# Stick-breaking attention: TensorE's products in the order of the source, the opening's V transposes between filling products, ScalarE's side steps tied to fixed places

## The chip, the core and the metric

The kernel runs as one program on one core of a Trainium2 chip. The metric is the device time of one execution in microseconds (us), as a median over runs. The core has five engines with a queue each: TensorE (PE; its weight loads stand apart as PEld), VectorE (DVE), ScalarE (ACT), GpSimd (POOL) and SyncE (SP), which issues most of the DMAs. An engine takes the instructions of its queue in the queue's order, and an instruction that waits on a semaphore holds up what stands behind it.

## The reference

One decoder layer over 1024 positions of width 1024, in float32. The input is normalized, scaled and shifted by a conditioning vector (adaLN), and projected once into all that follows. Two attention families run beside each other: native sparse attention (NSA) and stick-breaking attention; both are projected up, mixed by sigmoid gates, projected out and added; then comes an MLP. The change lies in the stick-breaking part:

```python
def stick_breaking_attention(q, k, v):
    ...
    def block(i):
        start = i * SB_QBLOCK
        t = start + jnp.arange(SB_QBLOCK)
        qb = lax.dynamic_slice_in_dim(q, start, SB_QBLOCK, axis=1)
        z = jnp.einsum('bqhd,bshd->bhqs', qb, k).astype(jnp.float32) * scale
        mask = key_pos[None, :] < t[:, None]
        log_keep = jnp.where(mask, jax.nn.log_sigmoid(-z), 0.0)
        suffix = lax.cumsum(log_keep, axis=3, reverse=True) - log_keep
        a = jnp.where(mask, jnp.exp(jax.nn.log_sigmoid(z) + suffix), 0.0)
        return jnp.einsum('bhqs,bshd->bqhd', a.astype(v.dtype), v)
```

So a weight is sigmoid(z) times the product of sigmoid(-z) over all later keys up to the query: a running product along each row of scores, for 8 heads of 64 channels.

## The kernel before, in words

**Stages.** Normalization, projections, NSA, stick-breaking, up-projection and gates, output projection, MLP. TensorE's operands are split into a high and a low part that it multiplies in separate products, so that three products make one of float32 accuracy. The last columns of the big input projection (the gates) aren't needed before the up-projection. They are cut into 28 units of 48 products (`unit_mm`, line 761, tiles `pd`, weights `uwh` and `uwl`), and their products fill TensorE between the dependent products of the two attention stages: the *filling products*, or fills. `drive` runs an attention generator and, after each step, takes as many fills as the step's cost times a ratio asks for; `pump` takes fills for a stretch of time. Line 1051 copies a finished unit out (`zo`), and line 63 and 66 split the next weights.

**Stick-breaking** (`sb_gens`). For each of 8 heads there are three groups of four chunks: the query blocks 3 to 0 with all their keys (512, 384, 256 and 128 columns), the blocks 7 to 4 with the 512 columns up to the diagonal, and the same blocks with the columns before (512, 384, 256 and 128). One step takes one chunk:
- TensorE makes the scores in a PSUM bank `psx`, of which there are three: Q with the high part of K (line 1156), with the low part (1157), and the causal mask as a further product (1159).
- ScalarE takes two sigmoids of the bank: `sig` (1161), and in place of the scores sigmoid(-z) (1162).
- VectorE runs the product along the row as a scan (1171, into `Pt`), one step later. The scan is what frees the `psx` bank. GpSimd multiplies `sig` by it (1173).
- A group later, TensorE transposes the weights (1188, into `pt`, two banks), ScalarE and VectorE split them into `th` (1196) and `tl` (1197), and TensorE multiplies them by V (1208, one bank `po`).
- At the end of a group of outputs, 1212 and 1214 add the two halves of `po`.

**Side work.** ScalarE, GpSimd and SyncE work beside this on 32 pieces of the MLP's adaLN weights (`ada_rest`: a DMA at line 436, a scaling on ScalarE at 456, an addition on GpSimd at 460). For the next head, Q is cast on ScalarE (1108), its lower half is corrected on GpSimd (1113), and K is split on GpSimd (63, 66). For each pair of heads TensorE transposes V (1126), and ScalarE and VectorE split it (1130, 1132).

**What sets the order.** A scheduler puts each engine's instructions in order when the program is built: of those that its model holds ready, it takes the one of highest priority. Edges added by hand that only order (no semaphore) bind it. `track` notes the last product of an attention step, and `behind` ties a fill behind it; before the change, that was done for one fill in six (`m % 6 == 0`). Everything else, the fills in between and ScalarE's side steps included, moved where the scheduler saw room. In the change, line numbers go up by 7 to 18 from line 427 on: the products of line 761 stand at 776, the scores at 1174, 1175 and 1177, the transposes at 1206, the V products at 1226, the Q cast at 1126, the V transposes at 1144, the adaLN scaling at 463.

Of the kernel before, what the change touches and what calls it, by code (L numbers as in the profile page):

```python
# [6 lines left out]
F32 = mybir.dt.float32  # L7
F32R = mybir.dt.float32r
BF16 = mybir.dt.bfloat16
AF = mybir.ActivationFunctionType  # L10
# [9 lines left out]
HD = 64  # L20
# [15 lines left out]
def build(tc, I, out):  # L36
    nc = tc.nc
# [74 lines left out]
    ones = const.tile([128, 128], F32, name="ones")  # L112
# [311 lines left out]
            nc.scalar.copy(csrc[which][:, h * 512:(h + 1) * 512], cb[which][h])  # L424


    def ada_rest(pool_, rows, ahead, engines, W=512):
        groups = [(r, h) for r in rows for h in range(D // W)]
        total = len(groups) * NK
        nxt = []  # L430

        def load(n):
            r, h = groups[n // NK]
            raw = pool_.tile([128, W], F32, name="adraw", bufs=ahead)
            c0 = (2 + r) * D + h * W
            nc.sync.dma_start(raw, ada_k[:, n % NK, c0:c0 + W])
            nxt.append(raw)

        for n in range(min(ahead, total)):
            load(n)  # L440
        yield
        for n in range(total):
            raw = nxt.pop(0)
            k = n % NK
            (r, h), w, e = groups[n // NK], cs[:, k:k + 1], engines[n // NK % len(engines)]
            if k == 0:
                acc = pool_.tile([128, W], F32, name="adacc", bufs=1)
            if e == "v":
                if k == 0:
                    nc.vector.tensor_scalar(acc, raw, w, None, op0=OP.mult)  # L450
                else:
                    nc.vector.scalar_tensor_tensor(acc, raw, w, acc, op0=OP.mult, op1=OP.add)
            else:
                d = acc if k == 0 else raw
                if e == "s":
                    nc.scalar.mul(d, raw, w)
                else:
                    nc.gpsimd.tensor_scalar(d, raw, w, 0.0, op0=OP.mult, op1=OP.add)
                if k:
                    nc.gpsimd.tensor_tensor(acc, acc, raw, op=OP.add)  # L460
            if n + ahead < total:
                load(n + ahead)
            if k == NK - 1:
                nc.sync.dma_start(acc_d[r][:, h * W:(h + 1) * W], acc)
            yield
# [271 lines left out]

    MM = 0.216

    last, free = [], [0]  # L740

    def track(ins):

        last[:] = [ins.ins]

    def behind(ins):

# [4 lines left out]
    def unit_mm(w, sink):  # L752
        wh, wl = w
        pend = None
        for h in range(2):
            sl = slice(h * 512, (h + 1) * 512)
            p = pd()
            m = 0
            for k in range(NK):
                for n, (a, b) in enumerate(((wh[:, k], uH(k, sl)), (wh[:, k], ul[:, k, sl]), (wl[:, k], uH(k, sl)))):  # L760
                    r = nc.tensor.matmul(p, a, b, start=(k == 0 and n == 0), stop=(k == NK - 1 and n == 2))  # L761
                    if m % 6 == 0:
                        behind(r)
                    m += 1
                    if m == 3 and pend:
                        sink(*pend)
                        pend = None
                    yield MM
            pend = (h, p)
        sink(*pend)  # L770
# [307 lines left out]
    def pump(fill, us):  # L1078

        free[0] = 1  # L1080
        while us > 0:
            m = next(fill, None)
            if m is None:
                break
            us -= m
        free[0] = 0


    def sb_gens(sp):
        zero = sp.tile([128, 128], F32, name="zero")[:, 0:1]  # L1090
        nc.vector.memset(zero, 0.0)

        def load(u, h):
# [5 lines left out]
        def load_v(p):  # L1099
            vr = sp.tile([128, S], F32, name="vr", bufs=1)  # L1100
            nc.sync.dma_start(vr, z_d[8 + p])
            return vr

        def prep(h, ld):

            qr, kr = ld
            Q = sp.tile([128, S], F32R, name="Q", bufs=2)
            nc.scalar.copy(Q, qr)
            yield
            Kh = sp.tile([128, S], F32R, name="Kh", bufs=2)  # L1110
            hi(Kh, kr, "g")
            yield
            nc.gpsimd.tensor_tensor(Q[HD:], qr[HD:], f(Q)[HD:], op=OP.subtract)
            yield
            yield
            Kl = sp.tile([128, S], F32R, name="Kl", bufs=2)
            lo(Kl, kr, Kh, "g")
            yield Q, Kh, Kl
# [29 lines left out]
        def sb_a(kind, chunk, ops, A, edges):  # L1148

            i, c0, c1 = chunk  # L1150
            Q, Kh, Kl = ops
            w = c1 - c0
            p = psx()
            qs = Q[:, i * 128:(i + 1) * 128]
            diag = kind != 2
            track(nc.tensor.matmul(p[:, :w], qs, Kh[:, c0:c1], start=True, stop=False))
            track(nc.tensor.matmul(p[:, :w], qs, Kl[:, c0:c1], start=False, stop=not diag))
            if diag:
                track(nc.tensor.matmul(p[:, w - 128:w], identr, diagr, start=False, stop=True))
            sig = sp.tile([128, w], F32, name="sigr" if kind == 1 else "sig%d" % w, bufs=5 if kind == 1 else 2)  # L1160
            nc.scalar.activation(sig, p[:, :w], AF.Sigmoid, scale=HD ** -0.5)
            nc.scalar.activation(p[:, :w], p[:, :w], AF.Sigmoid, scale=-(HD ** -0.5))
            A[i, kind] = (sig, c0)

            def fin():
                Pt = sp.tile([128, 640], F32, name="Pt", bufs=6)
                if diag:
                    nc.vector.memset(Pt[:, w:w + 1], 1.0)
                else:
                    nc.vector.tensor_copy(Pt[:, w:w + 1], edges.pop(i)[:, 0:1])  # L1170
                nc.vector.tensor_tensor_scan(Pt[:, 0:w][:, ::-1], p[:, 0:w][:, ::-1], zero.to_broadcast([128, w]),
                                             1.0 if diag else Pt[:, w:w + 1], op0=OP.mult, op1=OP.add)
                nc.gpsimd.tensor_tensor(sig, sig, Pt[:, 1:w + 1], op=OP.mult)
                if kind == 1:
                    edges[i] = Pt
            return fin, max(w, 256) * 2 / 2400.
# [41 lines left out]
        def sb_all():  # L1218
            lds = {0: (load(0, 0), load(4, 0))}
            vr = load_v(0)  # L1220
            ops = {}
            for r in prep(0, lds[0]):
                ops[0] = r
            V = []
            for c in prep_v(vr, V):
                yield c
            groups = [(h, kind) for h in range(8) for kind in range(3)]
            A, edges, late = {}, {}, []
            extra = []
# [143 lines left out]
    fill = fill_all()  # L1373
    pump(fill, 25.0)
    drive(nsa_all(), fill, 0.4, 0.05)
    pump(fill, 20.0)
    close(wp)
    close(at)
    close(bnp)
    close(kvp)  # L1380
    sp = pool("sb", "right")
    ada_steps = ada_rest(sp, (3,), 2, "s", 256)
    drive(sb_gens(sp), fill, 0.55, 0.08, TAIL)
    for _ in ada_steps:
        pass
    close(sp)
# [407 lines left out]
```

## Time and profile before

| | us |
|---|---|
| median of 3 runs (1702.85 to 1706.73) | 1703.29 |
| the profiled execution | 1704.85 |
| its span, first to last instruction | 1703.1 |
| stick-breaking stage within it, first setup steps to last V product | 612 to 847 |
| TensorE busy in the span | 1636.8 |
| TensorE busy in the 235 us of that stage | 218.29 |

Times in the views are microseconds from the start of the span. A matmul row gives its start, its duration and the operand shapes; durations of successive matmuls overlap, so the pace is read from the distance of their starts. The name in brackets behind a row is the event that ended the idle time just before it. The clock in a windows row is the share of TensorE's full clock that was granted, over that window.

### The profile page before, as it was taken

Reading aid. Unit: us, or ns where it says so; the run is one execution under the profiler, and the core shown is the slowest. Engines: PE = TensorE matmul, PEld = TensorE weight load, DVE = VectorE, ACT = ScalarE, POOL = GpSimd, SP = SyncE. Lnnn points to the kernel's source line nnn. Section 1 sums busy time; section 2 is a strip of 40 time slices with the busy share of each in tenths; the row PEclk is TensorE's granted clock in tenths of the full one; section 3 lists DMA queues with packets and bytes.
Section 4 is the critical chain, followed back from the end, with each engine's and each line's share of the span. In section 5 each row is a group of like instructions: output and inputs, shape, how many; then the busy total and the mean of one; then the engine's idle time right before and its main releaser. Section 6 shows DMA issues by size and latency. Waiting matters only on the chain.

```text
span 1703.1 us, 25878 instructions
## 1 busy us (share of the span) xinstructions
PE 1636.8 (96%) x8484; PEld 1377.4 (81%) x8484; DVE 1273.8 (75%) x2614; ACT 873.9 (51%) x1898; POOL 950.7 (56%) x837
## 2 busy tenths in 40 slices
PE   6999999999999989999999999989999999999998
PEld 5879888888888867878778887768788888888886
DVE  7698478778777557878655557569888888979897
ACT  6433476667666456766554435534444443454442
POOL 0021143434434268775326303399889897989897
PEclk9999999999999999999999999999999999999999
DMA  9465344444543474441187543855363554636232
GB/s 304 109 198 157 110 142 156 128 149 143 166 131 125 130 196 128 115 125 59 36 301 232 165 151 127 292 212 210 134 262 116 231 211 148 251 113 268 98 148 99
DMA packets 195103, 279.87 MB, mean 164 GB/s; under 512 B 19401, under 2 KB 145049, under 8 KB 186009
## 3 DMA queue, kind: packets, MB, share of 16 engines
q1 hardware_dynamic: 190744, 276.13, 48.8%
q10 hardware_dynamic: 4224, 2.10, 0.4%
q8 instruction: 67, 1.10, 0.3%
q14 instruction: 68, 0.55, 0.1%
HBM read 203.71 MB, written 39.86 MB: 143 GB/s over the span
## 4 chain that ended last, share of the span: by engine, by line
PE 73%; POOL 8%; DMA 6%; DVE 6%; issue 3%; ACT 3%; SPq 1%; POOLq 0%; DVEq 0%; ACTq 0%
PE pd L761 15%; PE psx L1734 10%; PE pd L1668 7%; PE pt L1668 5%; PE px L1357 5%; PE po L955 4%; PE px L1470 4%; PE po L1734 3%; POOL raw L1708 3%; PE pt L975 2%; PE psx L844 2%; DMA adraw<-in_ada_w_dram 2%; PE psx L845 2%; POOL wbl L1710 1%; PE psx L603 1%
## 5 line engine op out<-in xcount | busy, mean ns | idle before, releaser
L1737 DVE TENSOR_TENSOR acc<-acc,psx 128x512 f32<-128x512 f32 x288 | 178.7, 675 | 9.8 <-PE psx L1734 9.7
L761 PE MATMUL pd<-uh,uwh 128*128 128x512 f32 x448 | 181.2, 404 | 0.7 <-ACT zo L1051 0.7
L761 PE MATMUL pd<-ul,uwh 128*128 128x512 f32 x448 | 177.4, 396 | 0.0
L761 PE MATMUL pd<-uh,uwl 128*128 128x512 f32 x448 | 177.1, 395 | 0.0
L66 DVE TENSOR_TENSOR wl<-aw,wh 128x1024 fp32r<-128x1024 f32 x49 | 114.6, 2339 | 63.9 <-ACT wh L61 63.9
L1708 POOL TENSOR_TENSOR raw<-r 128x512 f32<-128x512 f32 x80 | 132.5, 1675 | 32.1 <-ACT r L1643 32.0
L1734 PE MATMUL psx<-wbl,rah 128*128 128x512 f32 x336 | 131.3, 391 | 5.9 <-POOL wbl L1710 4.6
L1734 PE MATMUL psx<-wbh,rah 128*128 128x512 f32 x336 | 130.6, 390 | 1.9 <-ACT wbh L1709 1.5
L1734 PE MATMUL psx<-wbh,ral 128*128 128x512 f32 x336 | 130.9, 390 | 0.1
L947 DVE TENSOR_TENSOR tl<-pt,th 128x512 fp32r<-128x512 f32 (+8 forms) x168 | 103.5, 619 | 32.9 <-ACT th L946 31.4
L946 ACT CAST th<-pt 128x512 fp32r<-128x512 f32 (+8 forms) x168 | 88.9, 533 | 68.2 <-PE pt L975 67.0
L1710 POOL TENSOR_TENSOR wbl<-raw,wbh 128x1024 fp32r<-128x1024 f32 x40 | 108.9, 2724 | 19.5 <-ACT wbh L1709 19.5
L63 POOL TENSOR_SCALAR uwh<-uwr 128x512 fp32r<-128x512 f32 x54 | 34.3, 645 | 136.0 <-PE pd L761 115.9
L1696 POOL TENSOR_TENSOR w<-w,grow 128x1024 f32<-128x1024 f32 x32 | 95.0, 2992 | 11.8 <-DVE aw L1624 11.8
L1709 ACT CAST rah<-raw 128x1024 fp32r<-128x1024 f32 x40 | 41.5, 1051 | 113.9 <-PE po L1734 60.7
L761 PEld LDWEIGHTS pd<-uh,uwl 128*128 128x128 f32 x448 | 84.9, 189 | 17.2
L761 PEld LDWEIGHTS pd<-uh,uwh 128*128 128x128 f32 x448 | 85.2, 190 | 14.9 <-ACT zo L1051 1.1
L901 POOL TENSOR_TENSOR pcx<-pcx,tot 128x64 f32<-128x64 f32 (+7 forms) x32 | 11.5, 359 | 153.5 <-ACT Pn L864 40.8
L761 PEld LDWEIGHTS pd<-ul,uwh 128*128 128x128 f32 x448 | 85.1, 190 | 14.0
L1668 PE MATMUL pd<-mth,wh 128*128 128x512 f32 x224 | 87.3, 390 | 0.9 <-ACT wh L61 0.9
L1668 PE MATMUL pd<-mth,wl 128*128 128x512 f32 x224 | 87.1, 389 | 0.9 <-DVE wl L66 0.9
L1668 PE MATMUL pd<-mtl,wh 128*128 128x512 f32 x224 | 87.2, 389 | 0.0
(359 smaller groups left out, 5326.3 us busy)
## 6 DMA issues: line engine op xcount, KB each, us to landing
mtl<-t_d SPq DMA_DIRECT2D x35, 1024.0 KB, 5.7
mth<-t_d SPq DMA_DIRECT2D x35, 1024.0 KB, 8.2
w<-in_mlp_w_dram SPq DMA_DIRECT2D x32, 512.0 KB, 5.5
z_d<-zo SPq DMA_DIRECT2D x56, 256.0 KB, 2.3
Pr<-Pn SPq DMA_DIRECT2D x112, 128.0 KB, 2.0
aw<-in_mlp_w_dram SPq DMA_DIRECT2D x28, 512.0 KB, 4.0
uwr<-in_w_in_dram SPq DMA_DIRECT2D x54, 256.0 KB, 3.2
adraw<-in_ada_w_dram SPq DMA_DIRECT2D x48, 256.0 KB, 3.1
```

The source lines that it names most:

```text
L66: (nc.vector if e == "v" else nc.gpsimd).tensor_tensor(dst, src, f(h), op=OP.subtract)
L761: r = nc.tensor.matmul(p, a, b, start=(k == 0 and n == 0), stop=(k == NK - 1 and n == 2))
L946: nc.scalar.copy(th[:rows, :w], p[:rows, :w])
L947: nc.vector.tensor_tensor(tl[:rows, :w], p[:rows, :w], f(th)[:rows, :w], op=OP.subtract)
L955: track(nc.tensor.matmul(po_[:, :256], w, tt[q][:rows, m * 256:(m + 1) * 256], start=(n == 0 and m == 0 and q == 0), stop=(n == last and m ...
L1357: nc.tensor.matmul(p, a, b, start=(k == 0 and n == 0), stop=(k == 3 and n == 2))
L1668: nc.tensor.matmul(bank[ft], a[:, k, fs], b[k], start=(k == 0 and m == 0 and not on), stop=(k == 3 and m == 2), skip_group_check=on)
L1696: nc.gpsimd.tensor_tensor(W2[c][j], W2[c][j], grow2, op=OP.mult)
L1708: nc.gpsimd.tensor_tensor(d, block(i0, j0, s), block(i1, j1, s), op=OP.add if sg > 0 else OP.subtract)
L1710: (nc.vector if e == "v" else nc.gpsimd).tensor_tensor(l.rearrange("p s n -> p (s n)"), src, f(h).rearrange("p s n -> p (s n)"), op=OP.sub ...
L1734: nc.tensor.matmul(p, a[:, s, qs], b[:, s], start=(s == 0 and n == 0), stop=(s == 1 and n == 2))
L1737: nc.vector.tensor_tensor(acc[:, t, ds_], acc[:, t, ds_], p, op=OP.add if sg > 0 else OP.subtract)
```

## The change

Five things change, all for the stick-breaking stage:
- **A strict order for TensorE.** While `strict` isn't None, each product of the stage, every fill included, is tied by an order-only edge behind the one before it in the source. The scheduler can't move them any more.
- **ScalarE's side steps.** The adaLN scaling and the Q cast are tied behind the last sigmoid that the source has issued (`behind_sig`).
- **The opening.** `pump` before the stage takes 4 us of fills in place of 20. Then the generator runs to its first two stops (after the loads and the preparation of head 0, and after V's transposes), with 8 us of fills behind each.
- **An early sigmoid.** One sigmoid of one column comes ahead of the preparation, so ScalarE's sigmoid table is loaded there.
- **Buffers.** The adaLN pieces get four buffers and are loaded four ahead, in place of two.

```diff
     def ada_rest(pool_, rows, ahead, engines, W=512):
...
                 if e == "s":
-                    nc.scalar.mul(d, raw, w)
+                    behind_sig(nc.scalar.mul(d, raw, w))
...
-    last, free = [], [0]
+    last, free, strict = [], [0], [None]
+
+    def chain(ins):
+
+        if strict[0] is not None:
+            if strict[0]:
+                after(ins, strict[0])
+            strict[0] = ins
 
     def track(ins):
 
         last[:] = [ins.ins]
+        chain(ins)
...
                     r = nc.tensor.matmul(p, a, b, start=(k == 0 and n == 0), stop=(k == NK - 1 and n == 2))
-                    if m % 6 == 0:
+                    if strict[0] is not None:
+                        chain(r)
+                    elif m % 6 == 0:
                         behind(r)
...
             Q = sp.tile([128, S], F32R, name="Q", bufs=2)
-            nc.scalar.copy(Q, qr)
+            behind_sig(nc.scalar.copy(Q, qr))
...
-            nc.scalar.activation(p[:, :w], p[:, :w], AF.Sigmoid, scale=-(HD ** -0.5))
+            sig_last[0] = nc.scalar.activation(p[:, :w], p[:, :w], AF.Sigmoid, scale=-(HD ** -0.5))
...
             vr = load_v(0)
+
+            nc.scalar.activation(warm, ones[:, 0:1], AF.Sigmoid)
             ops = {}
             for r in prep(0, lds[0]):
                 ops[0] = r
+            yield 0.0
             V = []
             for c in prep_v(vr, V):
-                yield c
+                pass
+            yield 0.0
...
-    pump(fill, 20.0)
+    pump(fill, 4.0)
...
-    ada_steps = ada_rest(sp, (3,), 2, "s", 256)
-    drive(sb_gens(sp), fill, 0.55, 0.08, TAIL)
+    ada_steps = ada_rest(sp, (3,), 4, "s", 256)
+    sb = sb_gens(sp)
+    strict[0] = False
+    for us in (8.0, 8.0):
+        next(sb)
+        pump(fill, us)
+    drive(sb, fill, 0.55, 0.08, TAIL)
+    strict[0] = None
+    sig_last[0] = None
```

**TensorE's queue at the opening.** Before, from the second chunk's scores of the first group on (`psx` are the scores, `pd` the fills):

```order
L1156 MATMUL psx<-Kh,Q 128x256
L1157 MATMUL psx<-Kl,Q 128x256
L1159 MATMUL psx<-diagr,identr 128x128
L761 MATMUL pd<-uh,uwl 128x512
L761 MATMUL pd<-uh,uwh 128x512
L761 MATMUL pd<-ul,uwh 128x512
L761 MATMUL pd<-uh,uwl 128x512
L1156 MATMUL psx<-Kh,Q 128x128
L1157 MATMUL psx<-Kl,Q 128x128
L1159 MATMUL psx<-diagr,identr 128x128
L1156 MATMUL psx<-Kh,Q 128x512
L1157 MATMUL psx<-Kl,Q 128x512
```

After, the same place:

```order
L1174 MATMUL psx<-Kh,Q 128x256
L1175 MATMUL psx<-Kl,Q 128x256
L1177 MATMUL psx<-diagr,identr 128x128
L776 MATMUL pd<-ul,uwh 128x512
L1174 MATMUL psx<-Kh,Q 128x128
L1175 MATMUL psx<-Kl,Q 128x128
L1177 MATMUL psx<-diagr,identr 128x128
L776 MATMUL pd<-uh,uwl 128x512
L1174 MATMUL psx<-Kh,Q 128x512
L1175 MATMUL psx<-Kl,Q 128x512
L1177 MATMUL psx<-diagr,identr 128x128
L776 MATMUL pd<-uh,uwh 128x512
```

Before, the fourth chunk (128 columns) is followed by three more sets of scores without a fill; after, one or two fills stand behind each set. Ahead of these rows, the eight V transposes stand 3 fills ahead of the first scores before, and 38 fills ahead of them after.

**ScalarE's queue at the opening.** Before, from the second Q cast on (that of head 1) to the first sigmoids:

```order
L1108 CAST Q<-zr 128x1024
L456 ACTIVATE adraw<-adraw,cs 128x256
L1130 CAST V<-pt 128x4x64 x2
L456 ACTIVATE adraw<-adraw,cs 128x256
L1130 CAST V<-pt 128x4x64 x2
L1161 ACT_TABLE_LOAD
L1161 ACTIVATE sig_8952<-psx 128x512
L1162 ACTIVATE psx<-psx 128x512
```

After, from the table load of the early sigmoid to the first sigmoids:

```order
L1240 ACT_TABLE_LOAD
L1240 ACTIVATE zero<-ones 128x1
L1068 COPY zo<-pd 128x512
L1126 CAST Q<-zr 128x1024
L1148 CAST V<-pt 128x4x64 x4
L1068 COPY zo<-pd 128x512
L1179 ACTIVATE sig_8945<-psx 128x512
L1180 ACTIVATE psx<-psx 128x512
```

Two adaLN scalings, which wait for DMAs and for GpSimd, have left the place ahead of the first sigmoid, and the table load stands ahead of Q.

**TensorE's queue in the steady state.** Before, in the middle of the stage, around the four transposes of one head's second group (the numbers tell tiles apart; `Kh_11287` is the K of the next head, `sigr` the weights of the older one):

```order
L1156 MATMUL psx_11617<-Kh_11287,Q_11255 128x512
L1157 MATMUL psx_11617<-Kl_11369,Q_11255 128x512
L1159 MATMUL psx_11617<-diagr_2056,identr_2043 128x128
L1156 MATMUL psx_11640<-Kh_11287,Q_11255 128x512
L1157 MATMUL psx_11640<-Kl_11369,Q_11255 128x512
L1159 MATMUL psx_11640<-diagr_2056,identr_2043 128x128
L1188 MATMUL pt_11435<-ident_71,sigr_11317 128x128
L1188 MATMUL pt_11435<-ident_71,sigr_11293 128x128
L1188 MATMUL pt_11435<-ident_71,sigr_11261 128x128
L1188 MATMUL pt_11435<-ident_71,sigr_11236 128x128
L1208 MATMUL po_11440<-th_11392,V_10888 128x128
L1208 MATMUL po_11440<-tl_11393,V_10888 128x128
```

After, around the same four transposes (`Kh_10928` is the K of the older head, to which `sigr` belongs):

```order
L776 MATMUL pd_11360<-ul_88,uwh_92 128x512
L1174 MATMUL psx_11421<-Kh_10928,Q_10883 128x128
L1175 MATMUL psx_11421<-Kl_11023,Q_10883 128x128
L776 MATMUL pd_11360<-uh_87,uwl_93 128x512
L1206 MATMUL pt_11432<-ident_71,sigr_11313 128x128
L1206 MATMUL pt_11432<-ident_71,sigr_11289 128x128
L1206 MATMUL pt_11432<-ident_71,sigr_11258 128x128
L1206 MATMUL pt_11432<-ident_71,sigr_11230 128x128
L1226 MATMUL po_11437<-th_11390,V_10885 128x128
L1226 MATMUL po_11437<-tl_11391,V_10885 128x128
L1226 MATMUL po_11437<-th_11411,V_10885 128x256
L1226 MATMUL po_11437<-tl_11412,V_10885 128x256
```

Before, the scheduler has moved the next head's scores ahead of these transposes, two sets of them back to back, and the fills come in longer runs elsewhere; after, the scores that stand there are the older head's last, and a fill stands between them and the transposes. Over the whole program the queue holds the same products in both; outside the stage and its opening they stand in the same order. Of the 64 mask products, 3 are followed directly by a fill before and 63 after; 37 are followed by a transpose before and 1 after; the other 24 before are followed by scores, V products or V's transposes.

## Rows read from the trace of the kernel before

**Rows 1.** The page's first part: busy us, share of the span, instructions.
```profile
PE 1636.8 (96%) x8484; PEld 1377.4 (81%) x8484; DVE 1273.8 (75%) x2614; ACT 873.9 (51%) x1898; POOL 950.7 (56%) x837
```

**Rows 2.** Windows of the stage and its neighbours, columns in the first line.
```profile
core 0: us, PE busy (x) PEld busy (x) DVE busy (x) ACT busy (x) POOL busy (x), PEclk, DMA share, GB/s
575.00:612.00 37.00, 35.98 (x200) 30.43 (x199) 14.64 (x27) 8.67 (x17) 10.51 (x11) 1.00 0.52 151
612.00:847.00 235.00, 218.29 (x1176) 180.91 (x1174) 176.97 (x341) 160.73 (x368) 156.31 (x163) 0.97 0.38 102
847.00:880.00 33.00, 32.81 (x145) 27.14 (x145) 13.80 (x15) 17.21 (x23) 1.03 (x1) 1.00 0.84 283
```

**Rows 3.** Windows within the stage.
```profile
612.00:630.00 18.00, 13.28 (x61) 10.87 (x60) 8.85 (x16) 13.04 (x29) 13.94 (x15) 0.81 0.75 201
630.00:650.00 20.00, 18.35 (x99) 15.62 (x98) 17.34 (x35) 16.20 (x39) 18.02 (x19) 0.91 0.33 90
650.00:675.00 25.00, 23.58 (x128) 18.80 (x127) 18.21 (x39) 17.24 (x42) 19.82 (x22) 1.00 0.58 150
675.00:700.00 25.00, 22.78 (x119) 19.04 (x120) 17.90 (x37) 16.55 (x37) 17.92 (x18) 0.93 0.41 115
700.00:725.00 25.00, 25.00 (x142) 21.33 (x142) 21.23 (x43) 19.09 (x45) 20.77 (x23) 1.00 0.48 125
725.00:750.00 25.00, 21.78 (x115) 17.38 (x114) 19.34 (x35) 17.66 (x41) 16.69 (x21) 1.00 0.53 141
```

**Rows 4.** TensorE's waits in 612 to 847: us in total, times, longest.
```profile
PE psx L1156 <- DVE Pt L1171: 11.0, 8, 4.7
PE pt L1188 <- DVE tl L1197: 2.4, 4, 0.9
```

**Rows 5.** Timeline of TensorE at the opening: start, duration, tiles, shapes, wait.
```profile
615.56 0.22 PE L1159 MATMUL psx<-diagr,identr 128*128 128x128 f32 x1
615.62 0.45 PE L761 MATMUL pd<-ul,uwh 128*128 128x512 f32 x1
615.90 0.40 PE L761 MATMUL pd<-uh,uwl 128*128 128x512 f32 x1
...
617.88 0.39 PE L761 MATMUL pd<-ul,uwh 128*128 128x512 f32 x1
618.11 0.39 PE L761 MATMUL pd<-uh,uwl 128*128 128x512 f32 x1
623.23 0.47 PE L1156 MATMUL psx<-Kh,Q 128*128 128x128 f32 x1 [4.72 <-DVE Pt L1171]
...
627.40 0.77 PE L761 MATMUL pd<-uh,uwh 128*128 128x512 f32 x1
```

**Rows 6.** Timeline of ScalarE at the opening.
```profile
616.35 0.51 ACT L456 ACTIVATE adraw<-adraw,cs 128x256 f32<-128x256 f32 x1 [1.23 <-DMA adraw<-in_ada_w_dram]
...
618.48 0.51 ACT L456 ACTIVATE adraw<-adraw,cs 128x256 f32<-128x256 f32 x1 [1.09 <-POOL adacc L460]
...
619.54 1.28 ACT L1161 ACT_TABLE_LOAD   x1
620.83 0.60 ACT L1161 ACTIVATE sig<-psx 128x512 f32<-128x512 f32 x1
```

**Rows 7.** Timeline of TensorE, filling products after a wait at 693.
```profile
694.29 0.63 PE L761 MATMUL pd<-ul,uwh 128*128 128x512 f32 x1
694.72 0.63 PE L761 MATMUL pd<-uh,uwl 128*128 128x512 f32 x1
```

**Rows 8.** Timeline of VectorE in steps of 512 columns.
```profile
766.62 1.22 DVE L1171 TENSOR_TENSOR_SCAN Pt<-psx,zero 128x512 f32<-128x512 f32 x1
767.76 0.66 DVE L1197 TENSOR_TENSOR tl<-pt,th 128x512 fp32r<-128x512 f32 x1
768.35 0.14 DVE L1170 COPY Pt<-Pt 128x1 f32<-128x1 f32 x1
768.74 1.22 DVE L1171 TENSOR_TENSOR_SCAN Pt<-psx,zero 128x512 f32<-128x512 f32 x1 [0.25 <-ACT psx L1162]
```

More of the change, by code (lines that the diff above doesn't have):

```diff
@@ L424, in build, with behind_sig @@
             nc.scalar.copy(csrc[which][:, h * 512:(h + 1) * 512], cb[which][h])
+    sig_last = [None]
+    def behind_sig(ins):
+        if sig_last[0]:
+            after(ins, sig_last[0])
     def ada_rest(pool_, rows, ahead, engines, W=512):
@@ L1089, in sb_gens @@
     def sb_gens(sp):
-        zero = sp.tile([128, 128], F32, name="zero")[:, 0:1]
+        zero = sp.tile([128, 128], F32, name="zero")
+        warm, zero = zero[:, 1:2], zero[:, 0:1]
         nc.vector.memset(zero, 0.0)
```

## The prediction

> **What bounds the kernel now.** The page's first part is read first: TensorE is busy for 96% of the span and no other engine for more than 75% [rows 1]. So the change can gain only where TensorE still loses time. The windows around the stage show where that is [rows 2]: the 37 us ahead of it are 35.98 busy, the 33 behind it 32.81, and the stage's own 235 us only 218.29. VectorE, ScalarE and GpSimd stand at 176.97, 160.73 and 156.31 there. TensorE bounds the stage, with 16.7 us idle.
>
> Idle time is not all of the loss. The smaller windows tell the rest [rows 3]: from 700 to 725 TensorE finishes 142 products in 25 us without a gap and at a granted clock of 1.00. Two other windows of 25 us in the stage do exactly that as well, the others shown 115 to 128. I take 142 in 25 us as the pace of this mix without a stall. The stage's 1176 products [rows 2] would then take 1176/142 × 25 = 207.0 us, so 28.0 of the 235 are lost:
> - idle: 235 − 218.29 = 16.7;
> - clock: the granted clock was 0.81, 0.91 and 0.93 in three windows [rows 3], which on their busy time is 0.19 × 13.28 + 0.09 × 18.35 + 0.07 × 22.78 = 5.8;
> - the remaining 5.5 is short delays between products that count as busy (an estimate by subtraction).
>
> The waits view names the idle time's largest item [rows 4]: 11.0 us in 8 waits of the score product for the scan that frees its PSUM bank, one of them 4.7. The timelines show that one. TensorE stops after the filling product at 618.11 and goes on at 623.23 with the fourth set of scores [rows 5]; no fill moves up in the meantime, though the next one stands a few products behind (627.40). The bank is late because the first sigmoid starts at 620.83 [rows 6], 5 us after the scores of its chunk were through (615.56). In between ScalarE does two adaLN scalings, which waited 1.23 for a DMA and 1.09 for GpSimd, the split of V, and the table load of 1.28 [rows 6]. After a stall the clock is down for a while: behind a wait at 693 the fills start 0.43 apart [rows 7], against 0.23 between 617.88 and 618.11 [rows 5]. That is 1.2 in place of 2.4 GHz.
>
> **The change, part by part.**
>
> *The opening.* The early sigmoid takes the table load away from the first chunk, `behind_sig` takes the two scalings away, the 38 fills ahead of the first scores (38 × 0.23 = 8.7 us) cover the preparation of head 0 and V's split. What was waited for is gone: 4.72 idle, and the 2.5 of clock in the first window. What is late next is the bank rotation: the fourth scores need the first bank's two sigmoids and its scan, about 0.5 + 0.5 + 1.22 us [rows 6, 8], while the second and third scores and five fills in between give about 1.9. I charge 0.4 there and 0.3 for the fifth, 0.7 together. The table load itself falls into a stretch in which ScalarE is busy for 8.67 of 37 us [rows 2], and costs nothing; if it delays the copy that follows it, at most its 1.28. The 16 us of fills that leave the stretch before the stage run inside it at the same 0.23 each: nothing.
>
> *The strict order.* No product is added or removed. Each step has its own fills now, so a bank that is freed late meets a fill in front of the product that wants it. I take the other 12.0 us of idle (16.7 − 4.72), the later clock losses (3.2) and the short delays as gone, and add two prices. First, 63 mask products are followed by a fill, against 3 before, and 1 by a transpose against 37. A fill behind a mask product starts 0.06 behind it (615.56 to 615.62), but the next fill comes 0.28 after (615.62 to 615.90), not 0.23 [rows 5]: 0.05 each. Some 25 mask products had such a follower before, and 63 have it now: 38 × 0.05 = 1.9 us. Second, a strict order can't jump over a product that waits, and ScalarE's side steps now sit at fixed places in the chain from sigmoid to transposes. Once a head a cast of Q, copies of a finished unit and of an output fall into one group. From below that costs nothing. From above it is one wait of 0.9 ((11.0 − 4.7)/7, the mean of the later waits for a scan [rows 4]) in each of the 24 groups: 21.6. I take one wait of the size that transposes show today, 2.4/4 = 0.6 [rows 4], for each of 8 heads: 5 us, since a group's weights have four steps from scores to transposes.
>
> *Side steps and buffers.* The scaling waited for a DMA; with four buffers and a fixed place behind sigmoids it is not at the head of a chain. The DMAs are the same. The first four are issued ahead of head 0's loads without a wait, and the 8 us of fills behind the loads cover them. Nothing, within the bounds above.
>
> The sum, against the profiled execution's own time: 207.0 + 0.7 + 1.9 + 5 = 214.6 in place of 235, 20.4 less. That execution took 1704.85 (span 1703.1, 1.75 around it), 1.56 above the median of 1703.29; so on the median 1703.3 − 20.4 = 1683. With the lower end of the second price: 209.6, and without the 0.7 as well 208.9, 26.1 less, 1677. With the upper end: 207.0 + 1.9 + 21.6 = 230.5, 4.5 less, 1699.
>
> **The rivals.**
>
> *No stall at all* (1677, worked out above). For it: three windows of 25 us run so today. Against: none longer does.
>
> *VectorE becomes the bound in wide steps.* In a step of 512 columns it needs a scan, a split and a copy of an edge: from 766.62 to 768.74 is 2.1 us a step [rows 8], 1.9 without the 0.25 in which it waited. TensorE's own share is six products of 512 columns at 0.23 (scores, V, two fills) and about five of 128 columns at a quarter of that, 1.7. With at most eight steps a head in which both are that wide or nearly so the excess is 8 × (1.9 − 1.7) = 1.6, rounded up to 1.8 for the waits, 14 over eight heads, in place of the 5: 224.0, 1692. For it: VectorE's 176.97 in 214.6 us would be 82% busy. Against: TensorE did 142 products with VectorE at 21.23 of 25 [rows 3].
>
> *The clock falls once a head.* Every head has a short wait, and TensorE runs at the lower clock after it. One such fall cost 1.6 (0.07 × 22.78, rows 3); 8 × 1.6 = 13 on top of the forecast: 1696. For it: 675 to 700 shows 0.93 with 2.22 us idle. Against: 650 to 675 and 725 to 750 kept 1.00 with 1.42 and 3.22 idle [rows 3]. The Trainium skill speaks for this rival: "TensorE: Matmul & The Clock Gate", section "A second HAM failure mode: psum-queue depth-cycling", tells of a kernel whose rotation through PSUM banks leaves TensorE short idle moments between groups, so that its clock goes up and down and throughput falls though each product at full clock is as fast as ever. By that rule it would come in every group; the trace agrees in one window of these three, which is why its chance is small.
>
> *The waits move and nothing is gained* (1703): the 28 us come back in other places, since the same sigmoid, scan and product chains feed TensorE.
>
> *Slower: the source's order pays at the transposes.* Before, the scheduler had moved scores of the next head ahead of transposes. In the strict order every transpose into one of two `pt` banks stands where the source has it, and may wait for the split (`tl`) of two steps ago; a waiting transpose now holds every fill behind it. At 0.6 us [rows 4] in the 64 of the 96 steps that are 512 or 384 columns wide, that is 38.4: 207.0 + 1.9 + 38.4 = 247.3, 12 more, 1715. It decides from 26.1/64 = 0.41 us a step. For it: only 4 such waits today, with the scheduler free to move. Against: the fills that stand between split and transposes are now in each step. That a wait holds fills is what the stop at 618 to 623 shows [rows 5]. The Trainium skill, same page, "Step-by-step: what each phase is for", says it as a rule: only weight loads are pulled ahead, products themselves stay in program order; the trace agrees, with 4.72 us in which no fill moved up.
>
> **How the numbers follow.** Chances: the forecast (1679 to 1688) 50%, no stall 13%, VectorE 17%, clock 8%, nothing gained 5%, slower 7%. A measurement of this kernel can tell 0.3%, 5 us, from no change; faster means below 1698.2. The first four cases lie there, 88%, of which I take 4 off for the ends of the VectorE and clock cases: 0.84. Same: 5% and 3 of these 4: 0.08. Slower: 7% and the last: 0.08. The range runs from 1673 (4 us below no stall, since 142 products in 25 us is itself an estimate of the pace) to 1700, just past the upper end of the second price; outside are most of "nothing gained", "slower", and little else.
>
> **What would show it.** Right: the stage is about 20 us shorter with the same number of products; the wait of 4.72 and the clock below 1.00 in the first window are gone; windows of 25 us with about 140 products throughout; the table load stands alone ahead of the stage. The second price shows as waits of `psx` or `pt` of under 1 us, about one a head. Wrong: waits for `tl` in most steps (slower), VectorE above 23 of 25 us in windows where TensorE has gaps, or a granted clock below 1.00 once in each head.

## The result, and the profile after

The changed kernel takes 1692.38 us (median of 4 runs, 1691.28 to 1694.78), beside 1704.57 of the kernel before in the same series. The ratio is 0.9926, with a 95% interval of 0.9910 to 0.9942: faster by 12.2 us. The forecast was 1683 with a range of 1673 to 1700; it said 20.4 less, so three fifths of that came. The time lies in the range, but not in the 1679 to 1688 that the forecast itself was given.

The profiled execution took 1691.28, with a span of 1689.5. Its first part answers [rows 1]; the windows answer [rows 2] and [rows 3], in the same columns:

```profile
PE 1626.5 (96%) x8484; PEld 1370.4 (81%) x8484; DVE 1269.7 (75%) x2614; ACT 874.2 (52%) x1899; POOL 944.9 (56%) x837
```

```profile
597.00:612.00 15.00, 12.56 (x59) 9.93 (x58) 6.45 (x17) 4.71 (x9) 8.58 (x7) 1.00 0.89 247
612.00:630.00 18.00, 14.76 (x66) 11.61 (x65) 7.64 (x15) 8.73 (x20) 9.90 (x9) 0.91 0.56 156
630.00:650.00 20.00, 18.61 (x109) 15.88 (x108) 16.74 (x33) 14.39 (x35) 16.75 (x20) 1.00 0.49 128
...
775.00:800.00 25.00, 25.00 (x143) 21.33 (x142) 21.13 (x44) 18.18 (x41) 17.83 (x18) 1.00 0.20 55
800.00:825.00 25.00, 25.00 (x144) 21.41 (x143) 20.45 (x39) 17.36 (x40) 11.57 (x14) 1.00 0.10 32
```

From 630 on every window has a granted clock of 1.00 and those of 25 us hold 136 to 144 products, where the kernel before had 115 to 142. The first two windows are poor.

**A measure that leaves the rest of the program out.** The executions differ by several us before the stage, where every engine's queue is still the same as in the kernel before. So I measure from the start of NSA's last product to the start of the last fill. The first fence is the kernel before, the second the changed one (TensorE's timeline):

```profile
595.84 0.28 PE L955 MATMUL po<-tl,vS 128*128 128x256 f32 x1
...
869.10 0.39 PE L761 MATMUL pd<-uh,uwl 128*128 128x512 f32 x1
```

```profile
596.09 0.28 PE L972 MATMUL po<-tl,vS 128*128 128x256 f32 x1
...
856.55 0.39 PE L776 MATMUL pd<-uh,uwl 128*128 128x512 f32 x1
```

That is 273.3 before and 260.5 after, 12.8 less. Both traces run the same products, so this gain can be split at equal work, counted in columns that TensorE has streamed since NSA's end: up to the work that the kernel before has done at 640 us, 0.6 of it came; behind that, 12.2. I call these the opening and the steady part. The forecast's terms split the same way: 4.72 + 2.5 − 0.7 = 6.5 for the opening, 20.4 − 6.5 = 13.9 for the steady part. So the steady part came nearly in full, and the opening not at all. The point of the split matters a little: between 636 and 655 us the changed kernel's opening comes out at 0.2 to 1.8, so opening and steady figures are good to about 1.5 us.

**Where the opening's gain went.** TensorE's waits from 580 to 850 (us in total, times, longest) answer [rows 4], and its timeline answers [rows 5]:

```profile
PE pt L1206 <- DVE tl L1215: 2.8, 3, 1.4
PE pt L1206 <- POOL sig L1191: 2.8, 1, 2.8
PE pt L1144 <- DMA vr<-z_d: 1.8, 1, 1.8
PE pt L1206 <- DVE Pt L1188: 1.4, 3, 0.7
PE po L1226 <- DVE tl L1215: 1.2, 1, 1.2
...
PE pt L1144 <- DVE V L1150: 0.5, 2, 0.2
```

```profile
606.84 1.06 PE L1144 MATMUL pt<-ident,vr 128*128 128x128 f32 x8 [1.76 <-DMA vr<-z_d]
...
619.49 0.33 PE L1174 MATMUL psx<-Kh,Q 128*128 128x128 f32 x1 [0.41 <-DVE Pt L1189]
...
621.25 0.39 PE L776 MATMUL pd<-ul,uwh 128*128 128x512 f32 x1
624.45 0.46 PE L1206 MATMUL pt<-ident,sig 128*128 128x128 f32 x1 [2.81 <-POOL sig L1191]
```

The stop of 4.72 before the fourth scores has become 0.41, as forecast. Two others came in its place: V's transposes wait 1.76 for their load, and the first transpose of weights waits 2.81 for GpSimd. ScalarE isn't the cause, in answer to [rows 6]: the table is loaded at 596.79, and the first sigmoid follows its scores at once (ScalarE's timeline).

```profile
596.79 1.28 ACT L1240 ACT_TABLE_LOAD   x1
...
617.09 0.60 ACT L1179 ACTIVATE sig<-psx 128x512 f32<-128x512 f32 x1 [6.68 <-PE psx L1177]
```

GpSimd's timeline (the first fence below) shows what held it. SyncE's timeline (the second) and the chain of waits (the third: start, us, what) show why:

```profile
610.58 1.06 POOL L63 TENSOR_SCALAR uwh<-uwr 128x512 fp32r<-128x512 f32 x1
619.86 1.04 POOL L63 TENSOR_SCALAR Kh<-zr 128x1024 fp32r<-128x1024 f32 x1 [8.21 <-DMA zr<-z_d]
620.98 2.37 POOL L66 TENSOR_TENSOR Kl<-zr,Kh 128x1024 fp32r<-128x1024 f32 x1
623.31 2.88 POOL L1191 TENSOR_TENSOR sig<-sig,Pt 128x512 f32<-128x512 f32 x4
```

```profile
603.80 1.72 SPq L443 DMA_DIRECT2D adraw<-in_ada_w_dram  x3
...
611.66 1.07 SPq L1069 DMA_DIRECT2D z_d<-zo  x1
612.82 1.10 SPq L1114 DMA_DIRECT2D zr<-z_d  x2
```

```profile
601.51 5.19 DMA vr<-z_d
...
613.32 6.36 DMA zr<-z_d
```

GpSimd has nothing to do from 611.6 to 619.8. The next instruction of its queue is the split of head 1's K, whose load SyncE issues only at 612.82, since `zr` has two buffers and head 0's K must be split before one is free. The load lands at 619.7; the two splits run; and head 0's first four products, for the first of which the scan was ready by 619.49 (it is what the fourth scores waited for), start at 623.31. The granted clock of 0.91 in 612 to 630 is the price behind the stop.

### The profile page after: what moved, and what is told of

Same layout as the page of the kernel before. It is cut to its first block, busy times and chain, and to the rows that moved or that the text cites. A ratio compares the mean times of both kernels' runs of the same rounds, so it can differ in the third digit from the quotient of the medians.

```text
span 1689.5 us, 25884 instructions
## 1 busy us (share of the span) xinstructions
PE 1626.5 (96%) x8484; PEld 1370.4 (81%) x8484; DVE 1269.7 (75%) x2614; ACT 874.2 (52%) x1899; POOL 944.9 (56%) x837
## 4 chain that ended last, share of the span: by engine, by line
PE 74%; POOL 8%; DMA 6%; DVE 5%; issue 3%; ACT 2%; SPq 1%; POOLq 0%; DVEq 0%; ACTq 0%
PE pd L776 16%; PE psx L1763 11%; PE pd L1697 7%; PE pt L1697 5%; PE px L1379 5%; PE po L972 4%; PE px L1499 4%; PE po L1763 3%; POOL raw L1737 3%; PE pt L992 2%; PE po L1226 2%; PE pt L1206 2%; PE psx L861 2%; PE psx L862 2%; PE cb L317 1%
## 5 line engine op out<-in xcount | busy, mean ns | idle before, releaser
L1737 POOL TENSOR_TENSOR raw<-r 128x512 f32<-128x512 f32 x80 | 132.4, 1673 | 32.1 <-ACT r L1672 32.0
L1189 DVE TENSOR_TENSOR_SCAN Pt<-psx,zero 128x512 f32<-128x512 f32 (+1 forms) x64 | 65.0, 1019 | 30.4 <-ACT psx L1180 28.6
```

Of the source, the lines that this page charges most:

```text
L1737: nc.gpsimd.tensor_tensor(d, block(i0, j0, s), block(i1, j1, s), op=OP.add if sg > 0 else OP.subtract)
```

## The experiments

Stage is the interval above; opening and steady are gains against the kernel before at equal work, from one profile each. Ratios are against the kernel before on the same chip.

| kernel | stage us | opening | steady | median us | ratio (95%) |
|---|---|---|---|---|---|
| before | 273.3 | | | | |
| changed | 260.5 | +0.6 | +12.2 | 1692.38 | 0.9926 (0.9910–0.9942) |
| changed, again | 262.2 | −0.9 | +12.0 | 1693.48 | 0.9941 (0.9923–0.9959) |
| e1, order alone | 268.4 | +0.1 | +4.8 | 1698.43 | 0.9962 (0.9948–0.9977) |
| e11, opening, early sigmoid and buffers alone | 283.5 | −1.6 | −8.6 | 1714.02 | 1.0051 (1.0032–1.0071) |
| e2, all but the order | 277.3 | +1.6 | −5.6 | 1709.25 | 1.0036 (1.0020–1.0053) |
| e4, all but the fixed side steps | 264.3 | +0.3 | +8.7 | 1697.14 | 0.9953 (0.9935–0.9970) |
| e5, all but the opening | 256.6 | +3.2 | +13.5 | 1686.97 | 0.9912 (0.9894–0.9930) |
| e7, all but the adaLN buffers | 259.7 | +1.5 | +12.0 | 1687.87 | 0.9902 (0.9882–0.9921) |
| e3, four Q and K buffers | 258.0 | +4.8 | +10.5 | 1687.28 | 0.9899 (0.9883–0.9915) |
| e8, GpSimd's splits moved back | 269.0 | +0.5 | +3.8 | 1700.37 | 0.9980 (0.9965–0.9995) |
| e6, e3 and fills 12 and 4 us | 252.9 | +7.0 | +13.3 | 1684.48 | 0.9893 (0.9871–0.9914) |
| e9, e5 and e3 | 254.5 | +5.3 | +13.5 | 1684.96 | 0.9878 (0.9856–0.9901) |
| e10, e9 without the early sigmoid | 255.2 | +4.6 | +13.5 | 1684.20 | 0.9872 (0.9850–0.9894) |

**e1: the order alone.** The kernel before with `chain` in `track` and `unit_mm` and

```diff
+    strict[0] = False
     drive(sb_gens(sp), fill, 0.55, 0.08, TAIL)
+    strict[0] = None
```

> The kernel before with one part of the change alone: every product of the stage tied in the source's order; the opening, ScalarE's side steps and the buffers as before. Theory A (the order gives the whole gain in the steady state, some 12 us between 640 and 840 us of the span, and the new opening gives nothing because GpSimd's first four products stand behind the next head's K split, whose load lands late): about 1692 to 1694, windows of 25 us with 137 to 144 products from 650 on, and the first set of waits about as in the kernel before (a stop of 4 to 5 us before the fourth or a later set of scores). Rival B (the order alone is worth the 20 forecast, and what is missing is the price of ScalarE's fixed places in every head): about 1687 or less.

Neither came: 1698.43 lies between the two numbers and the old time. The steady part gains 4.8, not 12. TensorE's waits for a bank are gone there, but transposes wait instead, up to 2.3 for `tl`, and ScalarE (640 to 850) stands still for adaLN loads, with splits and sigmoids behind it:

```profile
ACT adraw L456 <- DMA adraw<-in_ada_w_dram: 12.2, 9, 3.7
```

One such stop, and the longest wait of a transpose 7 us behind it (ScalarE's and TensorE's timelines):

```profile
686.61 0.51 ACT L456 ACTIVATE adraw<-adraw,cs 128x256 f32<-128x256 f32 x1 [3.65 <-DMA adraw<-in_ada_w_dram]
693.80 0.63 PE L1198 MATMUL pt<-ident,sig 128*128 128x128 f32 x4 [2.34 <-DVE tl L1207]
```

That the loads cause the waits is read from this order in time; no run changes the loads alone here. In the changed kernel no such wait of ScalarE is left. In the opening the stop has even grown, since the scalings, V's split and the table load stand ahead of the first sigmoid as before (TensorE's waits, 580 to 880):

```profile
PE psx L1166 <- DVE Pt L1181: 6.0, 1, 6.0
```

**e2: all but the order.** The changed kernel without `strict[0] = False`.

> The changed kernel without the strict order (one fill in six tied, as before); new opening, fixed side steps, early table load and four buffers kept. Theory A: the order is the whole gain, so 1702 to 1706, with waits for a PSUM bank as before spread over the stage. Rival B (the opening is worth its 6 us, the order the rest): 1696 to 1699. Rival C (side steps at fixed places alone remove the waits for the bank): 1692 to 1694, no different from the changed kernel.

All three missed: it is slower than before. Waits for a bank are spread over the steady part (640 to 850):

```profile
PE psx L1174 <- DVE Pt L1189: 6.8, 13, 1.2
```

So fixed side steps without the order are no gain; with it they are.

**e4: all but the fixed side steps.** In `behind_sig`:

```diff
-        if sig_last[0]:
-            after(ins, sig_last[0])
+        return
```

> The changed kernel with ScalarE's side steps (adaLN scaling and Q cast) left to the scheduler again, all else as changed. Theory A (the fixed places cost and give little in the steady state): within 3 us of the changed kernel, 1690 to 1695, the same windows from 650 on. Rival B (the fixed places are the price of 5 us that the forecast charged): 1687. Rival C (free side steps put DMA waits ahead of sigmoids, which a strict order can no longer jump over): 1698 or more, with ScalarE waiting for adaLN loads.

The median lies between A and C, at a ratio whose interval overlaps that of the changed kernel. The equal-work split gives 8.7 in the steady part against 12.0 to 12.2, some 3.4 less. B is out: the fixed places don't cost; by these profiles they give, which the ratios alone don't show. ScalarE waits 4.5 us in 4 waits for adaLN loads here.

**e11: opening, early sigmoid and buffers alone.** e2 with e4's edit.

> The kernel before with the rest of the change alone: new opening, early sigmoid, four adaLN buffers; neither the strict order nor the fixed side steps. Theory A (the new opening is worth nothing or less: V's load and GpSimd's queue give back what the first sigmoid gains): within 3 us of the kernel before, 1702 to 1708. Rival B (the forecast's term: the stop of 4.72 and its clock are worth 6.5): 1697 to 1699.

Both missed: it is slower than the kernel before, as e2 is, and their intervals overlap. The opening is 1.6 worse: left to the scheduler, the adaLN scalings run ahead of the first sigmoid again, and the fourth scores wait 6.3 us (580 to 880):

```profile
PE psx L1173 <- DVE Pt L1188: 16.9, 16, 6.3
```

In e2, which differs from e11 by the fixed side steps alone, the same scores wait 0.17 (TensorE's timeline). So it is the fixed places that take the long stop away:

```profile
614.76 0.33 PE L1174 MATMUL psx<-Kh,Q 128*128 128x128 f32 x1 [0.17 <-DVE Pt L1189]
```

Why the steady part of e2 and e11 is worse than that of the kernel before, which has the same freedom, I haven't settled: the scheduler makes another order of it, and only the waits for a bank can be seen.

**e3: four buffers for Q's and K's loads.**

```diff
-            zr = sp.tile([128, S], F32, name="zr", bufs=2)
+            zr = sp.tile([128, S], F32, name="zr", bufs=4)
```

> The changed kernel with four buffers in place of two for the loads of Q and K (tile zr), so that head 1's K can be loaded before head 0's is split. Theory A: the K split of head 1 runs during the fills ahead of the first scores, GpSimd's first product follows its scan within 1.5 us, the wait of 2.81 us before the first transpose shrinks below 0.5, the granted clock stays 1.00 there: 4 us less than the changed kernel, about 1688. Rival B: the first transpose waits for the sigmoid, scan and product chain itself; the wait stays above 2 us and the time within 1 us of the changed kernel.

A came: 1687.28, and 4.2 more in the opening than the changed kernel. GpSimd's timeline and the window show it:

```profile
611.82 1.06 POOL L63 TENSOR_SCALAR Kh<-zr 128x1024 fp32r<-128x1024 f32 x1 [1.28 <-DMA zr<-z_d]
612.96 2.39 POOL L66 TENSOR_TENSOR Kl<-zr,Kh 128x1024 fp32r<-128x1024 f32 x1
618.88 2.89 POOL L1191 TENSOR_TENSOR sig<-sig,Pt 128x512 f32<-128x512 f32 x4 [3.53 <-DVE Pt L1189]
```

```profile
612.00:630.00 18.00, 17.57 (x92) 14.27 (x91) 11.40 (x20) 12.78 (x30) 13.04 (x13) 1.00 0.97 242
```

The split runs while the fills do, the products wait only for their scan, the first transposes of weights don't wait, and the clock stays at 1.00: 92 products in that window in place of 66. V's transposes still wait for their load, 2.2 us.

**e8: the same place in GpSimd's queue, without an earlier load.**

```diff
-            hi(Kh, kr, "g")
+            r = nc.gpsimd.tensor_scalar(Kh, kr, 1.0, 0.0, op0=OP.mult, op1=OP.add)
+            if prod_last[0]:
+                after(r, prod_last[0])
...
-                nc.gpsimd.tensor_tensor(sig, sig, Pt[:, 1:w + 1], op=OP.mult)
+                prod_last[0] = nc.gpsimd.tensor_tensor(sig, sig, Pt[:, 1:w + 1], op=OP.mult)
```

> The changed kernel with one order-only edge more: the high split of the next head's K on GpSimd stands behind the last product (sig times Pt) that the source has issued, so head 1's split no longer stands ahead of head 0's first four products. Loads and buffers as changed. Theory A (the place in GpSimd's queue is the cause, the late load only its means): the wait of 2.81 before the first transpose falls below 0.7, and the time is 3 to 4.5 us below the changed kernel beside it. Rival B (the load's lateness matters by itself, or the chain from sigmoid to product is that slow): within 1 us of the changed kernel.

The cause is confirmed, and both times missed: the median is 6.9 above the changed kernel beside it. The first transpose no longer waits, but the split of 1.05 + 2.40 now falls between later products, and that of the next group waits longer than the first did (TensorE, then GpSimd):

```profile
621.46 0.27 PE L1208 MATMUL pt<-ident,sig 128*128 128x128 f32 x1
...
636.02 0.55 PE L1208 MATMUL pt<-ident,sigr 128*128 128x128 f32 x3 [3.89 <-POOL sigr L1193]
```

```profile
629.98 2.40 POOL L66 TENSOR_TENSOR Kl<-zr,Kh 128x1024 fp32r<-128x1024 f32 x1
632.33 1.22 POOL L63 TENSOR_SCALAR uwh<-uwr 128x512 fp32r<-128x512 f32 x2
633.50 3.52 POOL L1193 TENSOR_TENSOR sigr<-sigr,Pt 128x512 f32<-128x512 f32 x2
```

So moving the split back in this way doesn't mend GpSimd's order. What did, in e3, was to let it run in the stretch in which GpSimd is idle, and for that its data must be there.

**The changed kernel again**, beside e5, e6 and e8:

> The changed kernel itself once more, unedited, as the measure for the three that run beside it: 1690 to 1696, ratio to the kernel before 0.991 to 0.994.

As expected, at 0.9941. The same wait for GpSimd, 3.1.

**e5: all but the opening.**

```diff
-    pump(fill, 4.0)
+    pump(fill, 20.0)
...
-    for us in (8.0, 8.0):
-        next(sb)
-        pump(fill, us)
```

and `prep_v` yields its steps again.

> The changed kernel with the opening of the kernel before (20 us of fills ahead of the stage, none behind the generator's first two stops; V's transposes 3 fills ahead of the first scores); order, side steps, early table load and four buffers as changed. Theory A (the opening as changed is worth nothing, since GpSimd holds the first transposes anyway): within 2 us of the changed kernel beside it, and a wait of 2 to 4 us for GpSimd's first product. Rival B (the new opening is worth the 6 us of the forecast and something else eats them): 5 us or more slower than the changed kernel.

Both missed, on the good side: the new opening is not worth nothing, it costs. The median is 6.5 below the changed kernel beside it, and the stage is 3.9 to 5.6 us shorter with the old opening. V's transposes stand 16 us of fills behind NSA's end and don't wait for their load; the wait for GpSimd is there all the same, 3.4. And the stop before the fourth scores is as short as in the changed kernel, though V's transposes stand 3 fills ahead of the first scores again (TensorE's timeline):

```profile
617.63 0.33 PE L1174 MATMUL psx<-Kh,Q 128*128 128x128 f32 x1 [0.40 <-DVE Pt L1189]
```

So the 38 fills between the two weren't needed against the stop of 4.72; e10 below leaves out the early sigmoid too, and the stop is 1.14.

**e6: four Q and K buffers, and V's transposes 4 us later.** e3 with

```diff
-    for us in (8.0, 8.0):
+    for us in (12.0, 4.0):
```

> The changed kernel with four buffers for the loads of Q and K, and 12 and 4 us of fills at the opening's two stops in place of 8 and 8, so that V's transposes stand 4 us later while the first scores stay. Theory A: the wait for GpSimd (2.81) and the wait for V's load (1.76 to 2.2) are both gone; 6 to 7 us less than the changed kernel beside it, about 1686. Rival B: V's split then holds ScalarE ahead of the first sigmoid, a wait for a PSUM bank of 1 to 2 us comes in place: 4 to 5 us less, no better than with the four buffers alone.

A came, by more than it said: both waits are gone, and the median is 9.0 below the changed kernel beside it, not 6 to 7. The opening gains 7.0 where the forecast had 6.5, and the stage is 20.4 us shorter than in the kernel before.

```profile
597.00:612.00 15.00, 14.32 (x68) 11.61 (x67) 5.92 (x13) 4.65 (x9) 8.62 (x7) 1.00 0.88 231
612.00:630.00 18.00, 17.58 (x94) 14.31 (x93) 14.30 (x28) 14.34 (x34) 14.82 (x15) 1.00 1.06 276
```

**e7: the adaLN pieces two ahead.**

```diff
-    ada_steps = ada_rest(sp, (3,), 4, "s", 256)
+    ada_steps = ada_rest(sp, (3,), 2, "s", 256)
```

> The changed kernel with the adaLN pieces loaded two ahead in two buffers, as before, in place of four. Theory A (the forecast's term: the side steps sit behind sigmoids and no chain waits for their loads): within 2 us of the changed kernel, 1691 to 1695. Rival B (with fixed places a late adaLN load now holds the splits and sigmoids queued behind it on ScalarE, which the strict order can't step around): 1697 or more, with ScalarE waiting for adaLN loads in the waits view.

No slower: its median lies below A's 1691 to 1695. The interval of its ratio ends at 0.9921, just under the 0.9923 at which that of the changed kernel's repeat begins, and overlaps that of the first measurement, so whether it is faster is open. In its profile the wait for GpSimd is shorter by 1.1 us (580 to 880). Counted from NSA's last product, SyncE issues head 1's K 0.6 us earlier, with two adaLN loads in front of it in place of four, and the split starts 1.0 earlier.

```profile
PE pt L1206 <- POOL sig L1191: 1.7, 1, 1.7
```

B is out.

**e9: the old opening and four Q and K buffers.**

> The changed kernel with the opening of the kernel before and four buffers for the loads of Q and K. Theory A: the wait for GpSimd's first product (3.4 with the old opening) goes with the early load, and no wait for V's load is there; the stage comes to within 3 us of the forecast's 214.6 for the same work: 1681 to 1684, a ratio of 0.987 to 0.989. Rival B (one or the other only shifts the wait to the splits behind it): no better than either alone, 1686 to 1688.

A for the ratio, 0.9878; the median is 1 us past its upper end. The ratio's interval overlaps those of e3 and e5, so that the two gains add is shown only by the stage, 3.5 and 2.1 us shorter than theirs. No wait for V's load and none for GpSimd's first product is left; the longest is one of 1.9 for `tl`.

**e10: e9 without the early sigmoid.**

```diff
-            nc.scalar.activation(warm, ones[:, 0:1], AF.Sigmoid)
```

> The kernel with old opening and four load buffers, without the early sigmoid: the table load (1.28) falls between V's split and the first sigmoid. Theory A: the fourth scores wait about 1.3 us longer for their bank, and the clock may fall for a moment: 1 to 3 us more than the kernel beside it. Rival B: the fills ahead of the fourth scores hide it: within 0.5 us.

The fourth scores wait 1.14 in place of 0.41, and the time is the same: within the noise B, in the profile's 0.7 us half of A. By the profiles the early table load is worth under 1 us here.

e6, e9 and e10 beat both kernels, at 1684 to 1685 (e6 against the changed kernel's repeat beside it); their order among themselves is open.

## Why the prediction was right, and where its size was off

1. *TensorE bounds the stage, and its pace without a stall is 142 products in 25 us.* Right. Windows of 25 us without a gap hold 143 and 144 products, as the windows at 775 and 800 above show.
2. *The strict order takes away the spread waits, at 1.9 for mask products and 5 for fixed places.* Right in size: the steady part gained 12.2 of 13.9. The waits that are left from 630 to 840 add up to 5.9 (2.8 + 1.4 + 1.2 + 0.5 in the waits view of that stretch, nine in all), against the 5 charged for eight. The 1.9 was not measured by itself, and the rest of the difference is open. But the working laid it all to the order, with the fixed side steps as a price. The runs say otherwise: order alone 4.8, the change with free side steps 8.7, with fixed ones 10.5 to 13.5 (e8 aside, whose transposes wait longer later on too), without the order −5.6. In e1, the order alone, ScalarE's waits for adaLN loads stand ahead of TensorE's; with the fixed places those waits of ScalarE are gone.
3. *The opening is worth 6.5.* This is the term that was off; it measured +0.6 and −0.9. The step that failed reads "What was waited for is gone", with "the 38 fills ahead of the first scores cover the preparation of head 0 and V's split". They do, though e5 shows that the stop shrinks to 0.40 without them as well: it is the fixed side steps that take it away (0.17 in e2, 6.3 in e11), and the early sigmoid under 1 us of it (e10). But I followed ScalarE's chain only. Two others were late next. V's load is under way 5.4 us after the start of NSA's last product (601.51 − 596.09) and takes 5.2, so it lands 10.6 after it; only 34 fills stand between that product and the transposes, and TensorE is through with them after 9.0 (606.84 − 1.76 = 605.08). And head 1's K stood ahead of head 0's products in GpSimd's queue. The two waits, 0.41 for the bank and 0.09 × 14.76 = 1.3 of clock make 6.3, where 0.7 was charged. e3 and e6 give them back: 4.2 and 6.4 more in the opening than in the changed kernel. That the range held this miss was luck: its upper end had been drawn for waits in the steady part (and leaves out the 0.7, which would make it 1699.5).
4. *"The DMAs are the same ... Nothing"*, for the buffers. Nearly: e7 has 1.1 us less of the wait for GpSimd. The working had the first four adaLN loads ahead of head 0's loads. In the trace SyncE issues three of them at 603.80 and the fourth at 607.69, behind head 0's loads and V's (601.51) and ahead of head 1's K (612.82).
5. *The table load costs nothing where it stands.* Right, and by the profiles of e9 and e10 it gained under 1 us by moving.
6. *The rivals.* VectorE was not the bound: it was busy 21.13 of 25 us in a window that TensorE filled. The clock did not fall once a head; it was 1.00 from 630 on in this profile. The transposes waited for `tl` 3 times, not 64.

The time fell close to the VectorE rival's 1692, for another reason. That rival's number was no evidence for its mechanism.

## What to carry to other kernels

When a change takes the last wait out of an opening, write down for every queue what its next instruction is and when that one's data lands, also for work that belongs to a later step: here an early split with a late load held the four products behind it, and TensorE for 2.81 us. A missing buffer can be cheaper to add than a place in a queue to move: four buffers in place of two gave 4 us, moving the split cost 7. And try to fix the side work of the engines that feed a strictly ordered one together with it: here the order alone gave two fifths of the steady gain, and the rest of the change without the order a loss.

## What the runs showed that I had not expected

- Up to NSA's last product every engine's queue is the same in all these kernels, yet that product starts between 590.5 and 599.1 us in the 14 profiled executions. That spread is why the stage was measured by itself.
- A stop doesn't always cost the clock, and not always the same. After the 1.76 us at 606.84 the changed kernel's fills start 0.23 apart again from 607.97 on, and none of its windows behind stops of 1.4 us and less shows under 1.00. After the 2.81 us at 624.45 products of 512 columns start 0.43 apart, until about 628; in the repeat, after a like stop of 3.1, until about 632.5. And in e7 a stop of 1.7 us at 620, 4 us behind one of 0.41, did cost the clock, as its window shows where the 1.76 cost nothing. In the kernel before, the half clock of [rows 7] stands behind a stop of 1.33 and one of 0.61. What decides between these, the traces don't tell. The first fence is e7's window, the second TensorE's timeline of the kernel before:

```profile
621.00:626.00 5.00, 5.00 (x22) 4.11 (x21) 2.93 (x8) 3.41 (x8) 4.84 (x5) 0.72 0.40 98
```

```profile
691.87 0.44 PE L1156 MATMUL psx<-Kh,Q 128*128 128x384 f32 x1 [1.33 <-DVE Pt L1171]
...
693.16 0.90 PE L1188 MATMUL pt<-ident,sig 128*128 128x128 f32 x3 [0.61 <-DVE tl L1197]
```
